# A two-block transformer kernel: small tables on another queue, two opening transposes and the modulation sums read later, modulation items shifted within the first mixer

## The chip, the cores and the metric

The kernel runs on one NeuronCore of a Trainium2 chip. Its engines are TensorE (PE, with weight loads PEld), VectorE (DVE), ScalarE (ACT), GpSimd (POOL) and SyncE (SP, which here only issues DMAs). The metric is the device time of one execution in microseconds (us), and the median of several runs is what is compared.

## What is computed

Two transformer blocks are applied one after the other to 256 tokens of width 2048, in float32. Each block gets six modulation vectors from a conditioning vector `c`: shift, scale and gate for the mixer and for the feed-forward part. The core of the reference, shortened:

```python
# first block
mod = silu(c) @ w_ada + b_ada                      # 2048 x 12288
sh_m, sc_m, gt_m, sh_f, sc_f, gt_f = split(mod, 6)
h = rmsnorm(x, pre_mix_norm) * (1 + sc_m) + sh_m
proj = h @ w_in
y = concat([hgrn2(proj[..., :HG_COLS]), gated_delta(proj[..., HG_COLS:])]) @ w_out
x = x + gt_m * rmsnorm(y, post_mix_norm)
h = rmsnorm(x, pre_ffn_norm) * (1 + sc_f) + sh_f
x = x + gt_f * rmsnorm(square(relu(h @ w_ff1)) @ w_ff2, post_ffn_norm)
# second block
u = rmsnorm(x, norm_mix_g) * (1 + sc1) + sh1       # its own mod, from c_2 and ada_w_2
x = x + g1 * hybrid_mixer(u)                       # fox, nsa, dilated and differential attention
u = rmsnorm(x, norm_ffn_g) * (1 + sc2) + sh2
x = x + g2 * ((silu(u @ w_gate) * (u @ w_up)) @ w_down)
out = rmsnorm(x, final_norm_g)
```

The differential attention needs one number, the lambda: `exp(sum(l0*l1)) - exp(sum(l2*l3)) + 0.2`.

## The kernel before

The program writes out one order of instructions by hand, with a small clock model of its own (`_Clock`, line 75) that estimates when each engine would be done. The model only chooses the order; the engines then run their queues in order and wait on semaphores.

**Items.** All large weights come as an ordered list `items` of 512 KB pieces. SyncE fetches each into one of five `raw` buffers (`dma_to`), and a buffer is free for the next piece when the piece has been used. A weight piece is split by `prep`: ScalarE rounds it to `wh` (fp32r), VectorE (or GpSimd) takes the rest `wl = raw - wh`, and TensorE multiplies `wh` and `wl` with the activations. A modulation piece (`ada`) lies between the weights. In its plain form VectorE multiplies it by one entry of silu(c) and adds it to a sum `acc` (one instruction of 128x1024, 16 pieces to a sum). In the other form (`cg`) TensorE sums two pieces at a time.

**Where the modulation items lie.** `weight(k)` gives each weight piece of block `k` a number; within a phase the modulation items are dealt out in proportion to the running sum of the numbers, so that they are through 24 units before the phase's end. The first phase goes from the first mixer to `("oA", 3)`. It deals 96 modulation items: 64 of the plain form for the scale and shift of the first feed-forward part, and 32 of the `cg` form for the mixer's gate. Its blocks are, for half 0, the last two pieces of each of `hq hf hv hg`, the small `ab`, and `zq zk zv gg`; for half 1 eight pieces of each of the same eight; then four `oA` blocks of six pieces (the output projection).

**Blocks and fills.** `run(b)` emits the matmuls of a block. After each step of 128 weight rows (each second one where a block has 256 columns) `fill` emits one step of the generator at the head of the queue `pri` (the block's own evacuation), one of `urgent`, up to two of `fillers` (attention, HGRN and gated-delta generators) and some `prep`. At its start `run` empties `pri` down to one generator by force; a step that emits nothing then pulls a filler forward. The second half's evacuation of `hq` waits until the HGRN generator of half 0 is through (`hg_done`).

**Sums.** When a sum has its last piece, `fin` puts a reader on `urgent`: `col_gen` transposes it on TensorE and adds it up on ScalarE, `row_gen` spreads it over the partitions. The reader may start 0.2 us, on the program's clock, after the sum. There are two `acc` buffers.

**Opening blocks.** The first block of each feed-forward part (`f1` 0,0 and `ga` 0,0) has its result with tokens on the partitions; `ev_relu2_s` and `ev_gate2_s` take it out of PSUM for one tile of 128 tokens, yield twice, transpose it on TensorE, and go on with the second tile. All later blocks of the part are computed transposed and need no such step.

**Second mixer.** After `run_first(blocks["fv"], ...)` the program emits the small tables on SyncE's queue (`fbias`, `cw2`, `cpos`), the lambda's DMA, its two VectorE instructions, the exponential on ScalarE and two more on VectorE into `nlam`; then `cmp_pre` fetches two tables `w1` of 512 KB in rows of 256 bytes (tiles `S` in the trace) on SyncE's queue, and `run(blocks["qG"])` starts. `nlam` is first read by `diff_gen`, after the block `fdv`.

Of the kernel before, what the change touches and what calls it, by code (L numbers as in the profile page):

```python
# [13 lines left out]
AF = mybir.ActivationFunctionType  # L14
ALU = mybir.AluOpType
AX = mybir.AxisListType
ADD, SUB, MUL, MAX = ALU.add, ALU.subtract, ALU.mult, ALU.max
# [161 lines left out]
def two_blocks(ctx, tc, I, out):  # L179
    nc = tc.nc  # L180
    PSUM = bass.MemoryType.PSUM
    clk = _Clock()
    pe, dve, act, pool, sync = (_Eng(clk, n, e) for n, e in (
        ("pe", nc.tensor), ("dve", nc.vector), ("act", nc.scalar), ("pool", nc.gpsimd), ("sync", nc.sync)))
# [6 lines left out]
    def row_bcast(ap, n):  # L191
        return bass.AP(tensor=ap.tensor, offset=ap.offset, ap=[[0, 128], [1, n]])
# [20 lines left out]
    def wt(name="wt"):  # L213
        return w2.tile([128, 512], F32, name=name, tag="wt")
# [4 lines left out]
    def small(shape, tag):  # L219
        n = 1 if tag in ONE or tag[:2] in ("sp", "sq", "cm") else 2 if tag[-1] in "01" and tag[:2] in ("ss", "rk", "rq", "s1", "sv") else 4  # L220
        return sm.tile([128] + shape, F32, name=tag, tag=tag, bufs=n)
# [9 lines left out]
    accs = {}  # L231
# [189 lines left out]
    def pri_step():  # L421
        q = pri.popleft()
        try:
            next(q)
        except StopIteration:
            return
        pri.appendleft(q)
# [21 lines left out]
    def add(q, before=0.0):  # L449
        lead[q] = before  # L450
        fillers.append((clk.t["pe"], q))
# [54 lines left out]
    def banks():  # L506
        return [psg.tile([128, 512], F32, name="g", tag="g") for _ in range(2)]
# [55 lines left out]
    def add_acc(b, pts, out):  # L563
        for p, a, o in zip(pts, b.acc, out):
            dve.tensor_tensor(o, p, a, op=ADD)

    def run(b):
        while len(pri) > 1:
            clk.end = 0.0
            pri_step()  # L570
            if not clk.end:
                fill_step(True)
        pts = b.pts or banks()
        run_units(b, pts, b.idx, len(b.kts) - sum(items[i]["nk"] for i in b.idx))
        if b.acc:
            add_acc(b, pts, b.acc)
            add(b.done(b.acc))
        elif b.done:
            pri.append(b.done(pts))
# [69 lines left out]
    g = {"hp": hpool}  # L649
# [141 lines left out]
    def ada_vecs(blk, vs, key=None, mul=False, cg=False):  # L791

        if cg:
            groups = [((v, q),) for q in range(4) for v in vs]
        elif len(vs) == 2:
            groups = [tuple((v, q) for v in vs) for q in range(4)]
        else:
            groups = [((vs[0], q), (vs[0], q + 1)) for q in (0, 2)]
        for vq in groups:
            def fin(vq=vq):  # L800
                for v, q in vq:
                    at = clk.wr[clk.key(accs[blk, v, q][0])][0] + 0.2
                    urgent.append((at, col_gen(blk, v, q) if key is None else row_gen(blk, v, q, key, mul)))
            n = 8 if cg else 16
            for k in range(n):
                ADA.append((blk, vq, k, fin if k == n - 1 else None, key is not None, cg))
# [623 lines left out]
    def ev_relu2_s(pts):  # L1430
        new_r(0)
        for t in range(2):
            r = wt("relu")
            act.activation(r, pts[t], AF.Relu)
            dve.scalar_tensor_tensor(r, pts[t], 0.0, r, op0=MAX, op1=MUL)
            yield
            yield
            p = mx()
            for j in range(4):
                pe.transpose(p[:, j * 128:(j + 1) * 128], r[:, j * 128:(j + 1) * 128], ident)  # L1440
            h, l = (x[:, :, t * 128:(t + 1) * 128] for x in rT[0])
            p4 = p.rearrange("p (a b) -> p a b", a=4)
            act.activation(h, p4, AF.Copy)
            dve.tensor_sub(l, p4, h)
# [196 lines left out]
    def cmp_pre():  # L1641
        g["cx2"], g["cw1"], g["cslots"] = [], [], []
        for i in range(2):
            k, S = s_slot()
            g["cslots"].append(k)
            x2, w1 = S[:, 0:544].rearrange("p (g t) -> p g t", g=2), S[:, 544:1568].rearrange("p (l e) -> p l e", l=16)
            g["cx2"].append(x2)
            g["cw1"].append(w1)
            sync.dma_start(w1, I["nsa_cmp_w1_2"][0, i].rearrange("(l p) e -> p l e", p=128))
            pool.memset(x2[:, :, 255:272], 0.0)  # L1650

    def cmp_mid():
# [250 lines left out]
    def ev_gate2_s(pts):  # L1903
        for t in range(2):
            th = wt("th")
            act.activation(th, pts[t], AF.Tanh, scale=0.5)
            dve.scalar_tensor_tensor(th, th, 1.0, pts[t], op0=ADD, op1=MUL)
            yield
            yield
            p = mx()  # L1910
            for j in range(4):
                pe.transpose(p[:, j * 128:(j + 1) * 128], th[:, j * 128:(j + 1) * 128], ident)
            act.activation(g["sg2"][:, 0, :, t * 128:(t + 1) * 128], p.rearrange("p (a b) -> p a b", a=4), AF.Copy)
            yield
# [27 lines left out]
    def weight(k):  # L1942
        if k[0] in ("oB", "pB") or k == "fv" or k in (("f1", 0, 0), ("ga", 0, 0)) or k[:3] in (("f1", 0, 1), ("f2", 3, 2), ("f2", 3, 3)):
            return 0.0
        if k in ("qG", "kvH", "sv"):
            return 0.5
        return 1.0

    LOW = {k: 1 for k in ("qG", "kvH", "sv", "qA", "kB", "qC", "kD", "dv0", "dv1", "qE", "kF", "fdv")}
# [26 lines left out]
    for endkey, ntot in phases:  # L1976
# [5 lines left out]
        for k in order[lo:hi]:  # L1982
            b = blocks[k]
# [77 lines left out]
    for b, o in zip(wide[1:], ("hk", "hv", "hg", "oh1", "ol1", "oh2", "ol2")):  # L2061
        a = g[o] if o in g else oTp.tile([128, 2, 512], F32, name="part", tag=o)
# [137 lines left out]
    b = blocks["f2", 3, 3]  # L2200
# [30 lines left out]
    g["cw2"] = mp.tile([128, 128], F32, name="cw2")  # L2231
    g["cpos"] = mp.tile([128, 128], F32, name="cpos")
    g["cposT"] = mp.tile([128, 32], F32, name="cposT")
    sync.dma_start(g["fbias"], row_bcast(I["fox_f_bias_2"][0], 7))
    for i in range(2):
        sync.dma_start(g["cw2"][0:64, i * 64:(i + 1) * 64], I["nsa_cmp_w2_2"][0, i])
    sync.dma_start(g["cpos"][0:32], I["nsa_cmp_pos_2"][0].rearrange("i (a l) d -> (i a) (l d)", l=2))
    lam = wt("lam")
    lamp = lam[:, 256:384].rearrange("p (a d) -> p a d", a=2)
    lam = lam[:, 0:256]  # L2240
    sync.dma_start(lam, row_bcast(I["diff_lambda_2"][0], 256))
    lam4 = lam.rearrange("p (a b d) -> p a b d", a=2, b=2)
    lams = small([2], "lams")
    dve.tensor_tensor(lamp, lam4[:, :, 0], lam4[:, :, 1], op=MUL)
    dve.tensor_reduce(lams, lamp, axis=AX.X, op=ADD)
    act.activation(lams, lams, AF.Exp)
    dve.tensor_sub(g["nlam"], lams[:, 1:2], lams[:, 0:1])
    dve.tensor_scalar(g["nlam"], g["nlam"], -(0.8 - 0.6), None, op0=ADD)
    for i in range(3):
        oT[i] = tuple(oTp.tile([128, 4, T], FR, name=f"o2{a}{i}", tag=f"o{a}{i}") for a in "hl")  # L2250
    cmp_pre()
# [2 lines left out]
        run(blocks[n])  # L2254
    drain(lambda: g.get("nsa_done") == 4)
    run(blocks["qE"])
    run(blocks["kF"])
    drain(lambda: g.get("fox_done") == 4)
    g["fdv"] = cpool.tile([128, 2, 512], F32, name="fdv", tag="v4")
# [32 lines left out]
    b = blocks["pB", 0]  # L2292
# [64 lines left out]
    b = blocks["dn", 2, 3]  # L2357
# [48 lines left out]
```

## Time and profile before

| | |
|---|---|
| median of 3 runs | 2776.14 us (2774.57 to 2776.25) |
| the profiled execution | 2775.45 us, span 2773.7 us |
| TensorE busy | 2635.9 us, 95% |
| VectorE, ScalarE, GpSimd busy | 65%, 45%, 15% |
| moved by DMA | 643.59 MB, mean 232 GB/s |

The page of the profile shows the busy time of each engine and, in forty slices, how it is spread. The views used below are: busy time by stretch, with the TensorE clock that was granted (1.00 is 2.4 GHz, 0.50 is 1.2 GHz) and the share of time that the 16 DMA engines were busy; the list of waits; and the timeline of one engine, in which a bracket at the end of a row says how long the engine had been idle and what ended that. Nearly all instructions come from one helper and carry its line, L169, so rows are told apart by the names of tiles.

### The profile page before, as it was taken

Reading aid. Unit: us, or ns where it says so; the run is one execution under the profiler, and the core shown is the slowest. Engines: PE = TensorE matmul, PEld = TensorE weight load, DVE = VectorE, ACT = ScalarE, POOL = GpSimd, SP = SyncE. Lnnn points to the kernel's source line nnn. Section 1 sums busy time; section 2 is a strip of 40 time slices with the busy share of each in tenths; the row PEclk is TensorE's granted clock in tenths of the full one; section 3 lists DMA queues with packets and bytes.
Section 4 is the critical chain, followed back from the end, with each engine's and each line's share of the span. In section 5 each row is a group of like instructions: output and inputs, shape, how many; then the busy total and the mean of one; then the engine's idle time right before and its main releaser. Section 6 shows DMA issues by size and latency. Waiting matters only on the chain.

```text
span 2773.7 us, 39578 instructions
## 1 busy us (share of the span) xinstructions
PE 2635.9 (95%) x15073; PEld 2211.8 (80%) x15073; DVE 1808.2 (65%) x2245; ACT 1259.4 (45%) x2124; POOL 409.7 (15%) x264
## 2 busy tenths in 40 slices
PE   7998879999989999999999799998999999999998
PEld 4887768869758788887887698986768888888887
DVE  3567957764667777887855346567867756654566
ACT  3433344344554454444454336454454444443443
POOL 1000141231000000000001465663400000000001
PEclk9999989999999999999999999999999999999999
DMA  9977858782568988989965674667767777666664
GB/s 362 314 256 243 222 148 252 229 250 92 197 203 274 319 287 298 316 278 326 307 205 163 201 219 157 219 225 239 240 192 239 238 245 224 198 190 190 190 189 144
DMA packets 399806, 643.59 MB, mean 232 GB/s; under 512 B 31480, under 2 KB 198088, under 8 KB 398208
## 3 DMA queue, kind: packets, MB, share of 16 engines
q1 hardware_dynamic: 396528, 628.26, 71.2%
q10 hardware_dynamic: 2336, 10.42, 1.0%
q8 instruction: 118, 1.93, 0.3%
q0 software_dynamic: 752, 2.39, 0.2%
q14 instruction: 72, 0.59, 0.1%
HBM read 636.27 MB, written 4.19 MB: 231 GB/s over the span
## 4 chain that ended last, share of the span: by engine, by line
PE 56%; DMA 6%; DVE 5%; ACT 2%; issue 2%; POOL 1%; SPq 0%; ACTq 0%; POOLq 0%; DVEq 0%
PE g L169 53%; DMA raw<-in_w_ff_dram 4%; PE mx L169 3%; DVE wl L169 2%; ACT wh L169 2%; POOL wl L169 1%; DMA raw<-in_w_in_dram 1%; DVE acc L169 1%; DMA raw<-in_w_out_dram 1%; DVE y L169 1%; DVE xres L169 0%; DMA raw<-in_ffn_w_up_dram 0%; ACT S L169 0%; SPq L169 0%; DVE S L169 0%
## 5 line engine op out<-in xcount | busy, mean ns | idle before, releaser
L169 PE MATMUL g<-hT,wh 128*128 128x512 f32 (+1 forms) x4448 | 1221.4, 345 | 19.7 <-ACT wh L169 17.7
L169 ACT ACTIVATE wh<-raw 128x1024 fp32r<-128x1024 f32 (+2 forms) x793 | 823.4, 1045 | 903.8 <-PE g L169 447.9
L169 DVE TENSOR_TENSOR wl<-raw,wh 128x1024 fp32r<-128x1024 f32 x691 | 858.4, 1249 | 527.1 <-ACT wh L169 519.8
L169 PE MATMUL g<-hT,wl 128*128 128x256 f32 x3376 | 956.2, 283 | 18.4 <-DVE wl L169 12.5
L169 PEld LDWEIGHTS g<-hT,wh 128*128 128x128 f32 x4448 | 773.2, 191 | 145.6 <-issue 23.6
L169 PEld LDWEIGHTS g<-hT,wl 128*128 128x128 f32 x3376 | 644.5, 191 | 23.6 <-DVE wl L169 14.8
L169 DVE SCALAR_TENSOR_TENSOR acc<-raw,csil,acc 128x1024 f32<-128x1024 f32 x276 | 381.6, 1383 | 75.1 <-DMA raw<-in_ada_w_dram 72.3
L169 PE MATMUL g<-wh,rh 128*128 128x512 f32 x864 | 339.9, 393 | 0.0
L169 PE MATMUL g<-wl,rh 128*128 128x512 f32 x864 | 339.6, 393 | 0.0
L169 PE MATMUL g<-wh,rl 128*128 128x512 f32 x864 | 339.2, 393 | 0.0
L169 POOL TENSOR_TENSOR wl<-raw,wh 128x1024 fp32r<-128x1024 f32 (+2 forms) x102 | 238.0, 2343 | 210.2 <-ACT wh L169 192.5
L169 PEld LDWEIGHTS g<-wh,rl 128*128 128x128 f32 x864 | 162.8, 188 | 36.3
L169 PEld LDWEIGHTS g<-wh,rh 128*128 128x128 f32 x864 | 162.7, 188 | 36.0
L169 PEld LDWEIGHTS g<-wl,rh 128*128 128x128 f32 x864 | 162.8, 188 | 35.5
L169 PE MATMUL g<-wh,hT 128*128 128x512 f32 (+2 forms) x544 | 162.0, 369 | 2.5 <-DVE hk L169 2.2
L169 PEld LDWEIGHTS g<-wh,hT 128*128 128x128 f32 x544 | 98.0, 190 | 22.4 <-issue 8.9
L169 POOL TENSOR_TENSOR y<-yy,gw 128x512 f32<-128x512 f32 x6 | 7.6, 1292 | 711.5 <-DVE yy L169 711.5
L169 PE MATMUL g<-wl,hT 128*128 128x512 f32 (+2 forms) x272 | 98.7, 363 | 3.2 <-DVE wl L169 2.2
L169 POOL TENSOR_TENSOR y<-y,gw 128x512 f32<-128x512 f32 x6 | 9.6, 1625 | 552.2 <-DVE y L169 547.0
L169 PE MATMUL g<-raw,y 128*128 128x512 f32 (+1 forms) x192 | 83.9, 580 | 2.8 <-DVE y L169 2.6
L169 PE MATMUL ada<-raw,csil 128*32 128x512 f32 x384 | 64.2, 647 | 10.6 <-DMA raw<-in_w_ada_dram 9.0
L169 PEld LDWEIGHTS g<-raw,y 128*128 128x128 f32 x192 | 34.6, 190 | 36.8 <-issue 30.0
(453 smaller groups left out, 2583.4 us busy)
## 6 DMA issues: line engine op xcount, KB each, us to landing
raw<-in_w_ff_dram SPq DMA_DIRECT2D x256, 512.0 KB, 5.4
raw<-in_w_ada_dram SPq DMA_DIRECT2D x192, 512.0 KB, 5.7
raw<-in_ada_w_dram SPq DMA_DIRECT2D x192, 512.0 KB, 5.0
raw<-in_w_in_dram SPq DMA_DIRECT2D x176, 512.0 KB, 5.6
raw<-in_ffn_w_gate_dram SPq DMA_DIRECT2D x88, 512.0 KB, 4.5
raw<-in_ffn_w_up_dram SPq DMA_DIRECT2D x88, 512.0 KB, 4.7
raw<-in_ffn_w_down_dram SPq DMA_DIRECT2D x88, 512.0 KB, 4.4
raw<-in_w_out_dram SPq DMA_DIRECT2D x60, 512.0 KB, 5.0
```

Source lines behind the costliest of these rows:

```text
L169: r = f(out, *a, **kw)
```

## The change

The tables `fbias`, `cw2`, `cpos` and `w1` are issued on ScalarE's queue instead of SyncE's. The lambda becomes a generator among the fillers, added after block `qE`, with its DMA on ScalarE's queue and twelve yields between the DMA and the first use. Both opening evacuations yield seven times instead of twice before they transpose. Readers of plain sums may start 5.0 us after the sum instead of 0.2; for `cg` sums it stays 0.2. In the first phase the pieces of half 0 (and `ab`) weigh 0, those of `hq` and `hf` of half 1 0.5, those of `oA` 1.5, and all others 1 as before.

```diff
@@ ada_vecs
-                    at = clk.wr[clk.key(accs[blk, v, q][0])][0] + 0.2
+                    at = clk.wr[clk.key(accs[blk, v, q][0])][0] + (0.2 if cg else 5.0)
@@ ev_relu2_s, and the same in ev_gate2_s
-            yield
-            yield
+            for _ in range(7):
+                yield
             p = mx()
@@ cmp_pre
-            sync.dma_start(w1, I["nsa_cmp_w1_2"][0, i].rearrange("(l p) e -> p l e", p=128))
+            act.dma_start(w1, I["nsa_cmp_w1_2"][0, i].rearrange("(l p) e -> p l e", p=128))
@@ weight(k)
+        if k == "ab" or k[1:] == (0,) and k[0] in ("hq", "hf", "hv", "hg", "zq", "zk", "zv", "gg"):
+            return 0.0
+        if k in (("hq", 1), ("hf", 1)):
+            return 0.5
+        if k[0] == "oA":
+            return 1.5
         return 1.0
@@ the start of the second mixer
-    sync.dma_start(g["fbias"], row_bcast(I["fox_f_bias_2"][0], 7))
+    act.dma_start(g["fbias"], row_bcast(I["fox_f_bias_2"][0], 7))
     for i in range(2):
-        sync.dma_start(g["cw2"][0:64, i * 64:(i + 1) * 64], I["nsa_cmp_w2_2"][0, i])
-    sync.dma_start(g["cpos"][0:32], I["nsa_cmp_pos_2"][0].rearrange("i (a l) d -> (i a) (l d)", l=2))
-    lam = wt("lam")
...
+        act.dma_start(g["cw2"][0:64, i * 64:(i + 1) * 64], I["nsa_cmp_w2_2"][0, i])
+    act.dma_start(g["cpos"][0:32], I["nsa_cmp_pos_2"][0].rearrange("i (a l) d -> (i a) (l d)", l=2))
+    def lam_gen():
+        lam = wt("lam")
+        lamp = lam[:, 256:384].rearrange("p (a d) -> p a d", a=2)
+        lam = lam[:, 0:256]
+        act.dma_start(lam, row_bcast(I["diff_lambda_2"][0], 256))
+        for _ in range(12):
+            yield
+        lam4 = lam.rearrange("p (a b d) -> p a b d", a=2, b=2)
+        lams = small([2], "lams")
+        dve.tensor_tensor(lamp, lam4[:, :, 0], lam4[:, :, 1], op=MUL)
+        dve.tensor_reduce(lams, lamp, axis=AX.X, op=ADD)
+        act.activation(lams, lams, AF.Exp)
+        yield
+        dve.tensor_sub(g["nlam"], lams[:, 1:2], lams[:, 0:1])
+        dve.tensor_scalar(g["nlam"], g["nlam"], -(0.8 - 0.6), None, op0=ADD)
@@ after run(blocks["qE"])
+    add(lam_gen())
     run(blocks["kF"])
```

## Rows read from the trace of the kernel before

**Rows 1.** The page, busy us, share of the span and instructions by engine.
```profile
PE 2635.9 (95%) x15073; PEld 2211.8 (80%) x15073; DVE 1808.2 (65%) x2245; ACT 1259.4 (45%) x2124; POOL 409.7 (15%) x264
```

**Rows 2.** Busy time by stretch: us, engines, then PEclk, DMA share, GB/s.
```profile
205.00:360.00 155.00, 129.96 (x930) 119.93 (x929) 136.35 (x190) 61.24 (x126) 18.95 (x12) 0.94 0.80 236
360.00:402.00 42.00, 28.99 (x151) 24.90 (x150) 17.62 (x32) 16.01 (x53) 20.38 (x18) 0.72 0.31 84
402.00:485.00 83.00, 79.10 (x483) 67.65 (x482) 63.04 (x82) 37.94 (x81) 18.45 (x13) 1.00 0.87 247
...
205.00:402.00 197.00, 158.94 (x1078) 144.83 (x1077) 153.97 (x221) 77.25 (x179) 39.34 (x29) 0.90 0.69 203
402.00:620.00 218.00, 210.05 (x1430) 172.68 (x1429) 152.88 (x227) 92.57 (x206) 54.55 (x41) 1.00 0.83 242
```

**Rows 3.** The same view, of the instructions that read or write `acc`.
```profile
205.00:360.00 155.00, 2.40 (x16) 1.85 (x16) 46.19 (x37) 0.00 (x0) 0.00 (x0) 0.94 0.80 236
```

**Rows 4.** Waits, us in total, times, longest: SyncE's queue 205:402, TensorE 205:350.
```profile
SPq L169 <- DVE acc L169: 75.5, 35, 5.3
...
PE g L169 <- DVE wl L169: 12.9, 9, 4.1
```

**Rows 5.** Timeline around the hole in SyncE's issues, and the first `oA` copy.
```profile
368.06 0.37 SPq L169 DMA_DIRECT2D raw<-in_w_in_dram  x1
402.76 0.37 SPq L169 DMA_DIRECT2D raw<-in_w_ada_dram  x1
...
397.17 1.08 ACT L169 ACTIVATE hq<-g 128x512 f32<-128x512 f32 x2
...
683.79 1.07 ACT L169 ACTIVATE y<-g 128x512 f32<-128x512 f32 x2
```

**Rows 6.** Timeline of TensorE, ScalarE and SyncE at the second mixer's start.
```profile
1564.09 0.80 PE L169 MATMUL g<-hT,wh 128*128 128x256 f32 x2 [10.36 <-ACT wh L169]
...
1547.28 1.06 ACT L169 ACTIVATE wh<-raw 128x1024 fp32r<-128x1024 f32 x1 [4.74 <-DMA raw<-in_w_in_dram]
1560.93 0.20 ACT L169 ACTIVATE lams<-lams 128x2 f32<-128x2 f32 x1 [12.59 <-DVE lams L169]
...
1550.81 2.02 SPq L169 DMA_DIRECT2D raw<-in_w_in_dram  x4
1552.88 0.60 SPq L169 DMA_DIRECT2D fbias<-in_fox_f_bias_dram  x1
1553.52 1.21 SPq L169 DMA_DIRECT2D cw<-in_nsa_cmp_w_dram  x2
1554.77 0.61 SPq L169 DMA_DIRECT2D cpos<-in_nsa_cmp_pos_dram  x1
1555.43 0.42 SPq L169 DMA_DIRECT2D lam<-in_diff_lambda_dram  x1
1556.02 3.91 SPq L169 DMA_DIRECT2D S<-in_nsa_cmp_w_dram  x2
```

**Rows 7.** Busy time by stretch there, columns as in rows 2.
```profile
1554.00:1556.00 2.00, 0.00 (x0) 0.00 (x0) 0.00 (x0) 0.00 (x0) 0.00 (x0) 1.00 1.05 393
...
1558.00:1560.00 2.00, 0.00 (x0) 0.00 (x0) 0.00 (x0) 0.00 (x0) 0.00 (x0) 0.50 0.89 220
...
1568.00:1570.00 2.00, 2.00 (x12) 2.00 (x11) 2.00 (x3) 0.32 (x2) 0.66 (x1) 0.53 0.99 314
```

**Rows 8.** Timeline of ScalarE and TensorE at the two opening blocks' transposes.
```profile
796.71 1.06 ACT L169 ACTIVATE wh<-raw 128x1024 fp32r<-128x1024 f32 x1 [1.66 <-DMA raw<-in_w_ff_dram]
...
807.17 0.59 ACT L169 ACTIVATE relu<-g 128x512 f32<-128x512 f32 x1
...
809.30 1.12 PE L169 MATMUL mx<-c,relu 128*128 128x128 f32 x4 [5.99 <-DVE relu L169]
...
2053.60 0.66 PE L169 MATMUL mx<-c,th 128*128 128x128 f32 x4 [3.32 <-DVE th L169]
```

**Rows 9.** TensorE's waits over the whole span, for finished sums.
```profile
PE mx L169 <- DVE acc L169: 4.5, 3, 2.5
```

More of the change, by code (lines that the diff above doesn't have):

```diff
@@ L1907, in ev_gate2_s @@
             dve.scalar_tensor_tensor(th, th, 1.0, pts[t], op0=ADD, op1=MUL)
-            yield
-            yield
+            for _ in range(7):
+                yield
             p = mx()
@@ L2233, in two_blocks @@
     g["cposT"] = mp.tile([128, 32], F32, name="cposT")
-    sync.dma_start(g["fbias"], row_bcast(I["fox_f_bias_2"][0], 7))
+    act.dma_start(g["fbias"], row_bcast(I["fox_f_bias_2"][0], 7))
     for i in range(2):
-        sync.dma_start(g["cw2"][0:64, i * 64:(i + 1) * 64], I["nsa_cmp_w2_2"][0, i])
-    sync.dma_start(g["cpos"][0:32], I["nsa_cmp_pos_2"][0].rearrange("i (a l) d -> (i a) (l d)", l=2))
-    lam = wt("lam")
[L2239 to L2248, printed above, removed]
+        act.dma_start(g["cw2"][0:64, i * 64:(i + 1) * 64], I["nsa_cmp_w2_2"][0, i])
[12 more added lines that the diff above has]
+        act.activation(lams, lams, AF.Exp)
+        yield
+        dve.tensor_sub(g["nlam"], lams[:, 1:2], lams[:, 0:1])
+        dve.tensor_scalar(g["nlam"], g["nlam"], -(0.8 - 0.6), None, op0=ADD)
     for i in range(3):
```

## The prediction

> **What bounds the kernel now.** I read the page's busy line first: TensorE is busy 95% of the span, the other engines far less [rows 1]. Busy time alone has little to give back, so I looked for stages where TensorE is not busy or not at full clock: busy time by stage, then who waits for whom in it, then the timeline at each stop. Three places carry nearly all of it.
>
> The first is the opening of the first mixer's main loop, 205 to 402 us: TensorE is busy 158.94 of 197 us at a mean granted clock of 0.90 [rows 2]. That is 38 us idle, and 0.10 x 158.94 = 16 us of matmuls stretched by the half clock, 54 us in all. From 402 us on, up to 620, it is busy 210.05 of 218 at clock 1.00. In the opening VectorE is the fuller engine for most of the time: 136.35 of 155 us (88%) from 205 to 360. A third of that, 46.19 us in 37 instructions, is the modulation sums (`acc`) [rows 3]. The DMA queue shows the same: SyncE waits 75.5 us in 35 stops for VectorE to finish a sum before it may refill that raw buffer, and TensorE waits 12.9 us for low halves `wl` that VectorE makes [rows 4]. Then comes a stop of its own: SyncE issues nothing between 368.06 and 402.76 us, because the program runs out the HGRN chain before it goes on, and the gated-delta chain is emitted among it; ScalarE copies the second half's `hq` at 397.17 [rows 5]. In 360 to 402 the clock is 0.72.
>
> The second is the start of the second mixer: TensorE stands 10.36 us until 1564.09 because ScalarE's `wh` stand behind the exponential of the lambdas (1560.93), which stands behind a DMA that SyncE issued at 1555.43 [rows 6]. The third is two stops in front of transposes of the opening blocks, 5.99 and 3.32 us [rows 8]; three stops for finished sums add 4.5 us [rows 9].
>
> **Items shift within the first mixer.** No byte and no instruction is added. Working the weights through with the code: 96 sum items follow the first 64; the stage's weight falls from 81 to 68. Before, 21 of the 96 lie among half 0's blocks, 19 in `hq`, `hf` of half 1, 56 in `hv` to `gg`, none in `oA`. After: 0, 12, 68 and 16. So before `hv` of half 1, which starts near 402 us, 28 of 40 items go away: 28 x 1.25 us (46.19/37 [rows 3]) = 35 us less on VectorE, and 28 x 0.52 = 15 MB less to fetch. VectorE's 153.97 us in the opening become 119 [rows 2]. TensorE's own work at full clock is 0.90 x 158.94 = 143 us. With 119 beside 143, VectorE is 83% full; the nearest row is 402 to 485, VectorE 63.04 of 83 (76%), where TensorE lost 4 of 83 us, 5%. At 5 to 15% of 143 it loses 7 to 21 us in place of 54: a gain of 33 to 47, and I take 40. The stop at 368 to 402 goes with it because the HGRN and convolution steps, which queue on VectorE, end earlier than the weight blocks do; the chain's matmuls done in that stop are not saved, only laid between weight matmuls, and the 143 counts them.
>
> The 28 items come back later. Between 402 and 620 VectorE's 152.88 us grow by up to 35 to 188, or 86% of 218 [rows 2]. Its row for such a load is 205 to 360 (88%), where TensorE idled 25 of 155 us, 16%; that would cost 16% of 218 = 35 less the 8 lost there now, 27. But 16 of the items now lie in `oA`, and gate-vector items (32 of the 96) are summed by TensorE, not VectorE. I take a cost of 10, bounds 0 and 27. Net 30, bounds 6 and 47.
>
> **Lambdas and tables on ScalarE's queue.** The tables' six issues took 0.60, 1.21, 0.61 and 3.91 us on SyncE [rows 6], 6.3 us, which ScalarE now spends. It had ended a `wh` at 1548.34 and then stood for the exponential until 1560.93. So it would be through its issues at about 1554.7 and copy `fv` by 1555.7, which the old stall covers; without that cover those 6.3 us would be on the path. What is next late is the weights: four raw tiles were issued from 1550.81, 2.1 MB, and moved at 393 GB/s [rows 7], about 5.4 us, the first landing near 1555. Then one `wh` of 1.06 us and a low half: TensorE goes on near 1557 to 1560 instead of 1564, a gain of 4 to 7. Bounds: nothing, if the tables' 1.05 MB in small rows (220 GB/s in 1558 to 1560, when they moved) come first, 4.8 us; and 10.4 plus some 2 us of half clock, which lasted to about 1569.5 (0.53 in 1568 to 1570 [rows 7]). I take 6. The lambda's DMA, two VectorE and one ScalarE instructions move behind `qE`; twelve turns of the filler queue pass between issue and first use, one a fill at most, so nothing waits for its landing.
>
> The Trainium skill ("DMA: Bandwidth & Descriptors", section "Issuing engines are not separate DMA queues") says that transfers started by ScalarE and SyncE run on the same 16 engines and interleave, so a second issuer saves only issue time. The trace has the engines at a share of 1.05 while the four tiles moved [rows 7], so they had no room for tables beside them; by the rule alone this part gives 1 or 2 us and the sum would be 38 or 39 instead of 43.
>
> **Transposes later.** In `f1` the stop of 5.99 us ends at 809.30, when ScalarE's `relu` of the second token tile (807.17) and a VectorE product are through [rows 8]. Seven turns instead of two put the first tile's transposes at the end of the next block (8 fills) and the second tile's at the head of the one after, where `run` empties the queue by force. TensorE can use the stop for the block's remaining matmuls, whose weights `wh` began at 796.71 were long there. But the second tile is evacuated only at that eighth fill, so at the boundary TensorE waits for `relu` 0.59, the product 0.68 and what stands before them: 1.4 us at least, up to 4.6 with two `wh` and `wl` ahead. I take 3, a gain of 3. In the gate block likewise 3.32 against about 2: a gain of 1. Together 4; bounds -2 (both waits come back a little longer) and 9.3 (both gone).
>
> **Sums read later.** Column and row readers start 5.0 instead of 0.2 us, on the program's own clock, after a sum. That can remove at most the three stops of 4.5 us [rows 9]; TensorE has matmuls ready in each. A buffer is held longer, but the next user of the same buffer is 16 items on. I take 3; bounds -1 and 4.5.
>
> **Sum.** 30 + 6 + 4 + 3 = 43 us. The profiled execution took 2775.45 us (span 2773.7 and 1.75 around it), 0.7 under the median 2776.14. 2775.45 - 43 = 2732.4, against the median 2733; I say 2733.
>
> **Rivals.**
> - *The chain sets the opening, not VectorE.* The HGRN steps hand over between TensorE, VectorE and GpSimd; with VectorE free the blocks `hq`, `hf` come through faster and TensorE only waits longer for the same chain. For it: in 360 to 402 VectorE was busy 17.62 of 42 us and TensorE still stood [rows 2]. Against it: before 360 VectorE was 88% busy. The opening would then give back about half, 25 less 10 later; with 13 of the other parts 28 us or, with those at half, 20: about 2750 to 2756, I say 2753.
> - *The later stage pays all (slower).* From `hv` to the second `oA` block 84 items and 56 weight units, 73 MB, must come through five raw buffers that VectorE or TensorE empties. They now have from 402 to about 691: the first `oA` block, six of the eight units, is copied out at 683.79 [rows 5]. That is 289 us, and some 303 with the gated-delta matmuls that move in. At the 242 GB/s of 402 to 620 the bytes take 303 us, at the 236 of the VectorE-bound 205 to 360 [rows 2] 311: little or nothing is lost. The other side is 54 + 13 = 67 us at the very most, so from about 205 GB/s down (358 us, 69 more than 289) the kernel is slower; at 200 (367, 78 more) it takes 2787. For it: five buffers refill no faster than VectorE, fuller here than before, frees them. Against it: the share was 0.83 at 242 GB/s, and the second half of the stretch is not full of VectorE work.
> - *All at the upper bounds*: 47 + 12 + 9 + 4 = 72, 2704.
> - *It doesn't do what it says*: the program orders work by a clock of its own, and the later items are forced early by the two `acc` buffers, or stalls only change their name. Then within 5 us of 2776.
>
> **How the numbers follow.** Chances: forecast (2715 to 2745) 0.50; chain 0.24; upper bounds 0.10; no change 0.08; slower 0.08. From 2704 to 2772 all but the slower case, the no-change case and the tail below 2704 are held, about 0.80. About 0.2%, 5.5 us, is what a measurement of this kernel can tell from no change. Faster 0.84, same 0.08, slower 0.08.
>
> **What would show it.** In the new trace: `hq` of half 1 copied near 340 to 360 instead of 397; VectorE's sums before it down to about 12; no 34 us hole in SyncE's issues; clock near 1.00 from 205 on; VectorE 80 to 87% full in the two hundred microseconds behind, with TensorE still over 93% busy there. At the second mixer a stop of 3 to 6 us, ended by a weight DMA, not by the lambdas. In `f1` a stop of about 3 us at a block boundary. The forecast is wrong if the hole before `hv` stays, or if TensorE's waits for raw weights between `hv` and `oA` grow by more than 20 us.

## The result and the profile after

| | before | after |
|---|---|---|
| median | 2775.36 us (2774.15 to 2776.25) | 2759.52 us (2756.43 to 2761.39) |
| the profiled execution, its span | 2775.45, 2773.7 us | 2756.43, 2754.7 us |

The ratio is 0.9935, 95% interval 0.9923 to 0.9948: 16 us or 18 us faster, by medians or by ratio. The forecast was 43 us, 2733. The direction was right, the size well under half.

Busy time by stretch after, columns as in rows 2; the first three and the next two answer [rows 2], the last two are the opening up to the copy of `hq` of half 1 and the way from there to the first feed-forward part:

```profile
205.00:360.00 155.00, 140.53 (x1014) 130.54 (x1014) 121.42 (x187) 72.50 (x137) 33.84 (x24) 0.96 0.63 171
360.00:402.00 42.00, 37.79 (x193) 30.60 (x192) 32.94 (x38) 17.41 (x45) 14.17 (x9) 0.92 0.86 250
402.00:485.00 83.00, 81.01 (x620) 76.74 (x619) 73.28 (x93) 32.92 (x74) 24.11 (x15) 0.98 0.84 230
205.00:402.00 197.00, 178.32 (x1206) 161.13 (x1206) 154.36 (x224) 89.92 (x182) 48.01 (x33) 0.95 0.68 188
402.00:620.00 218.00, 204.15 (x1437) 174.01 (x1436) 166.66 (x242) 90.85 (x222) 63.79 (x46) 0.98 0.86 251
...
205.00:349.60 144.60, 132.90 (x978) 124.35 (x977) 114.69 (x175) 65.02 (x125) 29.82 (x21) 0.95 0.67 183
349.60:740.30 390.70, 366.52 (x2296) 307.16 (x2296) 270.57 (x388) 171.86 (x378) 92.76 (x68) 0.98 0.75 224
```

The same two stretches of the kernel before:

```profile
205.00:397.20 192.20, 154.27 (x1062) 140.85 (x1060) 153.06 (x219) 73.03 (x173) 38.44 (x29) 0.91 0.71 208
397.20:763.00 365.80, 352.48 (x2204) 294.14 (x2204) 230.41 (x341) 163.02 (x331) 75.91 (x60) 0.99 0.67 202
```

The timeline after, of the rows that answer [rows 5], [rows 6] and [rows 8]:

```profile
336.23 0.37 SPq L169 DMA_DIRECT2D raw<-in_w_ada_dram  x1
358.07 0.37 SPq L169 DMA_DIRECT2D raw<-in_w_in_dram  x1
...
349.65 1.11 ACT L169 ACTIVATE hq<-g 128x512 f32<-128x512 f32 x2
...
664.01 1.08 ACT L169 ACTIVATE y<-g 128x512 f32<-128x512 f32 x2
...
790.56 0.69 PE L169 MATMUL mx<-c,relu 128*128 128x128 f32 x2 [5.84 <-DVE relu L169]
...
1519.46 1.58 ACTq L169 DMA_DIRECT2D S<-in_nsa_cmp_w_dram  x2
1520.64 1.95 SPq L169 DMA_DIRECT2D raw<-in_w_in_dram  x4
...
1526.76 1.06 ACT L169 ACTIVATE wh<-raw 128x1024 fp32r<-128x1024 f32 x1 [3.60 <-DMA raw<-in_w_in_dram]
...
1527.87 0.39 PE L169 MATMUL g<-hT,wh 128*128 128x256 f32 x1 [4.31 <-ACT wh L169]
...
2041.33 0.90 PE L169 MATMUL mx<-c,th 128*128 128x128 f32 x3 [8.92 <-DVE th L169]
```

To see where the time went, the same event is looked up in each trace. Each number is the start of that copy on ScalarE minus its start in the kernel before, in us; the columns behind "after" are experiments told below. Each column is one execution, and executions of one kernel differ by some microseconds, so a step of 3 us in one column means little by itself; one that comes back in several columns means more.

| copy (start before) | after | items | tables | sums | transposes | both tiles |
|---|---|---|---|---|---|---|
| `hq` of half 1 (397.17) | -47.5 | -48.9 | +0.7 | -2.6 | +0.6 | -48.0 |
| first `oA` (683.79) | -19.8 | -16.7 | +0.8 | -3.3 | +0.2 | -15.7 |
| last of `f1` (1421.78) | -29.9 | -22.6 | +0.2 | -11.4 | +3.4 | -30.2 |
| last `dv` (1803.16) | -35.3 | -23.3 | -10.1 | -7.2 | +4.0 | -39.5 |
| last `qE` (1838.64) | -30.5 | -23.6 | -9.8 | -3.7 | +4.4 | -39.7 |
| `fdv` (1894.49) | -27.0 | -23.8 | -6.3 | -4.0 | +4.5 | -36.3 |
| first `th` of the gate block (2051.59) | -25.8 | -24.7 | -6.8 | -4.3 | +3.8 | -36.1 |
| last `y` of the first down-projection (2298.23) | -18.9 | -24.7 | -8.3 | -4.7 | +10.8 | -40.2 |

The "after" column is a ledger. The opening gives some 20 to 23 us, the sums in `f1` and `f2` another 7, the second mixer's start 5. At `dv` the kernel is 35 us ahead, not far from the forecast's 43. Then it loses: 8 us from `dv` to `fdv`, and 7 more at the gate block.

### The profile page after: what moved, and what is told of

It is laid out like the page before. It is cut to its first block, busy times and chain, and to the rows that moved or that the text cites. A ratio compares the mean times of both kernels' runs of the same rounds, so it can differ in the third digit from the quotient of the medians.

```text
span 2754.7 us, 39576 instructions
## 1 busy us (share of the span) xinstructions
PE 2629.3 (95%) x15073; PEld 2207.5 (80%) x15073; DVE 1814.2 (66%) x2247; ACT 1260.8 (46%) x2124; POOL 410.0 (15%) x262
## 4 chain that ended last, share of the span: by engine, by line
PE 59%; DMA 4%; DVE 4%; POOL 2%; issue 2%; ACT 2%; SPq 0%; POOLq 0%; ACTq 0%; DVEq 0%
PE g L169 56%; PE mx L169 3%; POOL wl L169 1%; DMA raw<-in_w_in_dram 1%; DMA raw<-in_w_out_dram 1%; DVE wl L169 1%; DMA raw<-in_w_ff_dram 1%; ACT wh L169 1%; DVE acc L169 1%; DVE y L169 1%; DVE xres L169 0%; DMA raw<-in_ffn_w_up_dram 0%; DMA raw<-in_ada_w_dram 0%; DMA raw<-in_ffn_w_gate_dram 0%; DVE S L169 0%
## 5 line engine op out<-in xcount | busy, mean ns | idle before, releaser
L169 PEld LDWEIGHTS g<-hT,wh 128*128 128x128 f32 x4448 | 772.9, 191 | 125.8 <-issue 18.9
L169 POOL TENSOR_TENSOR wl<-raw,wh 128x1024 fp32r<-128x1024 f32 (+2 forms) x100 | 230.1, 2311 | 222.7 <-ACT wh L169 211.2
```

The source lines that it names most:

```text
L169: r = f(out, *a, **kw)
```

## The experiments

Ratios are against the kernel before, run on the same chip beside it (medians there 2771 to 2776).

| kernel | ratio, 95% interval | median, us |
|---|---|---|
| items alone | 0.9914 (0.9895 to 0.9933) | 2752.1 |
| tables and lambda alone | 0.9981 (0.9969 to 0.9994) | 2769.6 |
| sums alone | 0.9984 (0.9973 to 0.9996) | 2770.6 |
| transposes alone | 1.0036 (1.0023 to 1.0049) | 2785.4 |
| changed, old transposes | 0.9924 (0.9901 to 0.9947) | 2752.1 |
| and sums split | 0.9894 (0.9871 to 0.9917) | 2742.7 |
| and both tiles at once | 0.9864 (0.9839 to 0.9889) | 2734.1 |
| and lambda early | 0.9844 (0.9822 to 0.9867) | 2728.2 |
| before, sums narrow on the chip | 0.9956 (0.9939 to 0.9972) | 2760.7 |
| before, sums narrow in the clock | 0.9949 (0.9931 to 0.9967) | 2758.5 |
| before, narrow in both | 0.9916 (0.9901 to 0.9931) | 2748.4 |
| and fetched narrow | 0.9940 (0.9923 to 0.9956) | 2754.4 |
| before, fillers ahead | 1.0099 (1.0085 to 1.0114) | 2803.0 |
| lambda early, fillers ahead | 0.9969 (0.9959 to 0.9979) | 2766.4 |
| the same, old item weights | 0.9995 (0.9982 to 1.0008) | 2773.0 |
| items alone, sums narrow in the clock | 0.9938 (0.9919 to 0.9956) | 2756.8 |
| lambda early, sums narrow in the clock | 0.9841 (0.9821 to 0.9861) | 2729.8 |

**Each part alone.** Four kernels take over one part of the change each; their edits are hunks of the diff above.

Items:

> The kernel before with only the new weights for the modulation items. Theory A (each part has its own price, and the ledger by stage of the changed kernel's trace holds them): the first oA copy comes 18 to 22 us earlier, the first feed-forward part begins 20 to 24 us earlier, and the time is 2751 to 2757. Theory B (the forecast's 30 is right for this part, and something else eats it later in the changed kernel): the feed-forward part begins 28 to 33 us earlier, 2743 to 2748.

Tables and lambda:

> The kernel before with only the tables and the lambda moved to ScalarE's queue and the lambda made a later generator. Theory A (the lost ten microseconds of the second mixer belong to the late sums): the gain at the second mixer's start, 6 us, stays to the end: 2769 to 2771. Rival C (they belong to the lambda's generator, which runs among the kF block's attention steps): the gain of 6 us is gone again by the block after kF, and the time is 2775 to 2779.

Sums:

> The kernel before with only the later readers of plain sums (5.0 instead of 0.2). Theory A: 5 to 8 us gained in the first block's feed-forward part, where TensorE no longer stops for sums, and 5 to 10 us lost in the second mixer, where the readers fall among the attention steps: 2773 to 2781. Rival C (the second mixer's loss isn't theirs): 2768 to 2771.

Transposes:

> The kernel before with only seven yields instead of two in both opening evacuations. Theory A (the second tile of the gate block is now evacuated at the head of the next block, behind four weight roundings): about 0 in f1 and 5 to 7 us lost at the gate: 2780 to 2783. The forecast's value: 4 us gained, 2772. Rival C (the stop only changes its name, weights are what is late at both places): 2775 to 2777.

By the medians the four are worth 22, 4, 3 and -11 us (against 2773.97): 18 together, and the whole change 16 to 18. So the parts add up, within intervals of some 3 to 5 us either way for each. Theory A of the expectations holds for the first three in the places of gain and loss; for the sums its time does not (2770.6 lies in rival C's range). The transposes cost more than any theory had: 3 us stand by the end of `f1`, and 7 more at the gate block.

In the table of events the sums gain 8 us between `oA` and the end of `f1`, and lose 8 from there to `qE`: both places of theory A. The lambda's rival C is partly right too: from `qE` to `fdv` the tables' column falls from -9.8 to -6.3, with TensorE waiting 3.8 us for attention's VectorE steps in the `kF` block. The table repeats this in each kernel that has the lambda behind `qE` (after, tables, both tiles: 3.4 or 3.5 us lost there) and in no other (items, sums, transposes: 0.1 at most).

**The gate's transposes and the second mixer's sums, in the changed kernel.**

```diff
@@ ev_relu2_s, ev_gate2_s (old transposes, on the changed kernel)
-            for _ in range(7):
-                yield
+            yield
+            yield
```

> The changed kernel with both opening evacuations back at two yields. If the later transposes cost here what they cost alone (11 us on the kernel before), the stop before the gate block's second transposes falls from 8.9 us to about 3, and the time is 2746 to 2751. If the cost belongs to their meeting with the other parts, nothing is regained: 2757 to 2760.

2752.1 us, between the two expectations and nearer the first. That is 7 us less than the changed kernel by the medians and 3 by the ratios, whose intervals overlap. In the traces the loss of the gate block (7 us from its first `th` to the last `y`) is gone and the stop there is 2.29 us instead of 8.92, so that loss was the transposes'; the 11 us that they cost alone are not all regained.

```diff
@@ ada_vecs (sums split, on top)
-                    at = clk.wr[clk.key(accs[blk, v, q][0])][0] + (0.2 if cg else 5.0)
+                    at = clk.wr[clk.key(accs[blk, v, q][0])][0] + (0.2 if cg or blk == 1 and v in (2, 4, 5) else 5.0)
```

> The same, and the readers of the sums that finish in the second mixer and after it (scale of its feed-forward part, g1 and g2) may start 0.2 after the sum again, those before keep 5.0. If the late readers cost the second mixer its stop of 5.3 us before the kD scores, that stop falls under 2 us, and the time is 4 to 8 us under the kernel with old transposes: 2740 to 2745. If the lambda's generator is the cause, it is the same as that kernel within 2 us.

2742.7 us: 9 us less, and the stop before the `kD` scores goes from 5.44 us in the kernel with the old transposes to 0.50. This is that stop in the changed kernel, TensorE, then VectorE and GpSimd ahead of it:

```profile
1775.28 1.04 PE L169 MATMUL mx<-kD,qC 64*128 64x128 f32 x3 [5.33 <-DVE S L169]
...
1766.50 2.35 DVE L169 TENSOR_TENSOR colt<-red,cols 128x4 f32<-128x4 f32 x1
1768.88 2.27 DVE L169 SCALAR_TENSOR_TENSOR Affn<-colt,cols 128x4 f32<-128x4 f32 x1
1771.07 1.27 DVE L169 SCALAR_TENSOR_TENSOR acc<-raw,csil,acc 128x1024 f32<-128x1024 f32 x1
1772.27 2.29 DVE L169 TENSOR_TENSOR colt<-red,cols 128x4 f32<-128x4 f32 x1
...
1766.08 5.04 POOL L169 TENSOR_TENSOR wl<-raw,wh 128x1024 fp32r<-128x1024 f32 x2 [0.60 <-ACT wh L169]
1771.56 2.98 POOL L169 TENSOR_TENSOR wl<-raw,wh 128x1024 fp32r<-128x1024 f32 x1 [0.43 <-ACT wh L169]
```

and with the sums split:

```profile
1768.84 0.84 PE L169 MATMUL mx<-kD,qC 64*128 64x128 f32 x3 [0.50 <-DVE S L169]
```

In the changed kernel the late readers stand in VectorE's queue in front of the scores, and three of their four 128x4 instructions last until GpSimd's subtraction beside them ends.

**Both tiles at once.**

```diff
@@ ev_relu2_s (ev_gate2_s alike)
-        for t in range(2):
+        rs = []
+        for t in range(2):
             r = wt("relu")
             act.activation(r, pts[t], AF.Relu)
             dve.scalar_tensor_tensor(r, pts[t], 0.0, r, op0=MAX, op1=MUL)
+            rs.append(r)
+        for _ in range(4):
             yield
+        for t, r in enumerate(rs):
             yield
```

> The same, and the opening evacuations take both token tiles out of PSUM at once, then yield, then transpose the first and at the next step the second. If the stops of 5.8 and 3.3 us come from the second tile's evacuation standing behind the next block's weight roundings on ScalarE, both vanish, the next weights are late instead by up to 4 us in all, and the time falls by another 4 to 8 us: 2733 to 2740. If weights are what is late there anyhow, the stops only take their name, and the time stays within 2 us.

2734.1 us, another 9 less. These are TensorE's transposes, each row the first of its group, and none has a bracket: the stops (5.67 and 2.19 us in the kernel before this step, 5.84 and 8.92 in the changed kernel) are gone, and TensorE has no other stop in their place. On ScalarE both `th` (x2) now stand ahead of the roundings:

```profile
785.41 0.60 PE L169 MATMUL mx<-c,relu 128*128 128x128 f32 x4
...
2019.13 0.49 PE L169 MATMUL mx<-c,th 128*128 128x128 f32 x3
...
2022.39 0.38 PE L169 MATMUL mx<-c,th 128*128 128x128 f32 x2
...
2015.51 1.06 ACT L169 ACTIVATE th<-g 128x512 f32<-128x512 f32 x2
2016.46 2.05 ACT L169 ACTIVATE wh<-raw 128x1024 fp32r<-128x1024 f32 x2
```

**Lambda early.**

```diff
     add(fox_pre())
+    add(lam_gen())
...
     run(blocks["qE"])
-    add(lam_gen())
```

> The kernel with both tiles evacuated at once, and the lambda's generator added at the start of the second mixer instead of behind qE. If its steps cost the kF block the 3 us that the stage lost with the tables alone (9.8 us ahead after qE, 6.3 after fdv), that loss goes and the time falls by 2 to 4 us against the kernel with both tiles. If the lambda's exponential stands in ScalarE's queue ahead of weights at the mixer's start again, it is 3 to 6 us slower. If neither, within 1.5 us.

2728.2 us, the fastest of all here by its median. The intervals of this and the last kernel overlap, so for the whole time the place of the lambda is not shown to matter. For its stretch the traces show it. From the copy of `qE` to that of `fdv` the five kernels with the lambda behind `qE` take 59.3 to 59.5 us (after, tables, old transposes, sums split, both tiles). All others take 55.4 to 56.0, whether the lambda is where it was before or early, but for this one, which takes 56.9: its wait in the `kF` block fell only from 4.0 to 3.2 us.

**What bounded the opening.** The forecast said VectorE. To part its time from the order of the steps, the first sums are narrowed to 64 columns on the chip, in the program's clock, or in both. Where they are narrow on the chip, the kernel leaves out the other 960 columns of these sums, so its result is incomplete; it serves for its time alone.

```diff
@@ prep (all three; it counts the plain pieces)
+            st["plain"] = st.get("plain", 0) + 1
             if k == 0 and not it["row"]:
                 dve.tensor_scalar(a, it["raw"], sc, None, op0=MUL)
+            elif st["plain"] <= 40:
...
@@ narrow on the chip alone
+                nc.vector.scalar_tensor_tensor(a[:, 0:64], it["raw"][:, 0:64], sc, a[:, 0:64], op0=MUL, op1=ADD)
+                clk.run("dve", "scalar_tensor_tensor", a, [it["raw"], sc, a], [])
@@ narrow in both
+                dve.scalar_tensor_tensor(a[:, 0:64], it["raw"][:, 0:64], sc, a[:, 0:64], op0=MUL, op1=ADD)
@@ narrow in the clock alone
+                nc.vector.scalar_tensor_tensor(a, it["raw"], sc, a, op0=MUL, op1=ADD)
+                clk.run("dve", "scalar_tensor_tensor", a[:, 0:64], [it["raw"][:, 0:64], sc], [])
@@ dma_to (fetched narrow, on top of narrow in both)
+                if not it["cg"] and k and st["fetched"] <= 40:
+                    sync.dma_start(raw[:, 0:64], src[:, 0, 0:64])
```

On the chip alone:

> The kernel before, with 38 of the first 40 VectorE sum instructions reduced to 64 of their 1024 columns (the rest of these sums is left out, so the first feed-forward part's modulation is incomplete); all bytes are still fetched, all instructions keep their order. This takes some 42 us from VectorE in the opening and nothing from the DMA engines. If VectorE's time is what bounds the opening, hq of half 1 is copied at 345 to 360 instead of 397 and the time falls by 30 to 40 us, to 2735 to 2745. If the raw buffers' bytes bound it, hq comes at 385 or later and the time is over 2765; if the HGRN hand-overs bound it, in between.

In both:

> As the narrow sums (same sums left out beyond their first 64 columns, all bytes fetched, SyncE's order unchanged), but now the program's own clock also counts them as narrow, so it emits the HGRN and gated-delta steps earlier. If the order that the clock made was what kept hq of half 1 behind in the narrow sums (387 instead of the 350 of the changed kernel), hq comes at 345 to 362 and the time falls below 2750. If the bytes of the 28 items set it, hq stays at 380 to 390 and the time within 5 us of the narrow sums' 2760.

In the clock alone:

> The kernel before with all sums computed in full, but the program's clock counts the first 38 as narrow: only the order in which the steps are emitted changes, neither VectorE's work nor bytes. If VectorE's time and the order both count, hq of half 1 comes 5 to 20 us earlier than 397 and the time falls by 3 to 12 us. If the order alone decides, it falls by as much as with the narrow sums in both. If VectorE's time alone decides, within 3 us of the kernel before, or slower.

In both, and the pieces fetched narrow as well:

> As narrow in both, and of these 38 pieces only 64 of 1024 columns are fetched too (what is left out is the same): the bytes of the first 40 sum pieces all but vanish, 18 MB less. If bytes bound the opening, hq of half 1 comes at 340 to 355 here where narrow in both leaves it at 380 or later. If not, the two differ by less than 8 us at hq.

Busy time by stretch, first narrow on the chip alone:

```profile
205.00:360.00 155.00, 136.95 (x989) 125.48 (x988) 110.29 (x205) 66.53 (x147) 20.29 (x18) 0.96 0.85 253
360.00:402.00 42.00, 32.53 (x150) 28.26 (x148) 14.80 (x25) 18.96 (x46) 18.72 (x15) 0.63 0.22 62
```

SyncE's issues in it:

```profile
356.48 0.37 SPq L169 DMA_DIRECT2D raw<-in_w_in_dram  x1
393.05 0.37 SPq L169 DMA_DIRECT2D raw<-in_w_ada_dram  x1
```

and busy time by stretch, narrow in the clock alone:

```profile
205.00:360.00 155.00, 132.69 (x938) 122.50 (x936) 135.88 (x194) 62.02 (x127) 18.37 (x13) 0.94 0.81 237
360.00:402.00 42.00, 35.90 (x159) 27.20 (x159) 33.78 (x38) 23.28 (x65) 19.31 (x14) 0.92 0.92 251
```

On the chip alone the result lies between the readings of its expectation; in the clock alone `hq` came 34 us earlier, more than the 5 to 20 expected. With 26 us less work on VectorE up to 360 (110.29 against 136.35 [rows 2]), TensorE gains 7 us there, but the hole of SyncE stays (36 us) and the stretch from 360 to 402 is as bad as before. With VectorE as full as before and only the order of the steps another, that stretch is mended. Each is worth some 12 to 14 us, both together 23: on the kernel before the two causes add, within the intervals. `hq` comes at 387 (on the chip), 363 (in the clock) and 353 (in both). Fetching 18 MB less on top brought nothing (2754.4), so no run here shows the bytes to be the bound. It does not exclude them either: the order of steps shifts in that kernel too, the hole is back (34 us) and `hq` comes at 381, so the expected 8 us at most was missed.

Does simply emitting those steps sooner do it?

```diff
@@ fill_step (on the kernel before)
-            if force or at <= clk.t["pe"] + lag[0]:
+            if force or at <= clk.t["pe"] + (6.0 if "gg" in g and "hg_done" not in g else lag[0]):
```

> The kernel before, unchanged but for one rule of the emission: until the HGRN generator of half 0 is through, a filler step may be emitted up to 6 us before the program's clock calls it ready, instead of 0. No sum, no byte and no item moves, and SyncE's order is the same. If the opening's stop exists because these steps are written behind the weight work and then run out by force, SyncE's hole of 34 us goes or shrinks below 15, hq of half 1 comes 25 to 45 us earlier and the time falls by 12 to 25 us. If the narrow model gained for another reason (its sums' places), the hole stays and the time is within 5 us of the kernel before.

> The kernel with old item weights undone nowhere: both tiles evacuated at once, sums split, lambda early, new item weights, and the same 6 us rule. The changed kernel's own hole of 21 us before 358 and its stop of 6.0 us for hgA should shrink; if they do and nothing is late next, the time is 2 to 10 us under the kernel with the early lambda. If the steps now stand in front of weight work on VectorE, it is the same or up to 5 us slower.

> The same without the new item weights (the modulation items lie as in the kernel before). If the shift of the items mostly bought an order of steps, this is within 8 us of the same kernel with the new weights; if moving VectorE's 35 us is worth most of it, it is 12 to 25 us slower than that.

No. In the first the hole is gone and `hq` comes 24 us earlier, and yet it is 27 us slower: TensorE now stands in front of the steps themselves. Its wait for `hq` on VectorE from 205 to 402 us is new, that for `wl` was 14.2 us before; and up to 360 its granted clock is 0.80, where it was 0.94 [rows 2]:

```profile
PE mx L169 <- DVE hq L169: 12.9, 5, 5.6
PE g L169 <- DVE wl L169: 10.9, 13, 2.2
...
205.00:360.00 155.00, 117.10 (x692) 105.09 (x691) 103.92 (x148) 46.39 (x92) 18.39 (x15) 0.80 0.55 167
```

The rule spoils the fastest kernel too (2766.4), and with it the old and the new item weights are 7 us apart, which by the expectation speaks for the order of steps as most of what the shift bought. But both kernels lost much to the rule itself, so this is weak evidence. Neither the hole nor the time of `hq` is a price by itself: emitting the steps 6 us ahead removes the hole and loses more elsewhere. The expected gain of 12 to 25 us did not come. Whether a smaller lead would gain was not tried.

Last, whether the shift has already bought the order:

> Only the new item weights, as in the items alone (0.9914 of before), and the program's clock counts the first 38 full sums as narrow, which on the old item order gave 0.9949 by the order of steps alone. If the shift of the items bought the opening by the order of steps that it let the clock make, the two don't add: 0.990 to 0.993, 2746 to 2756. If it bought it by VectorE's time, they add: about 0.986, 2735 to 2740.

> The kernel with both tiles evacuated at once, sums split, early lambda and new item weights (0.9844 of before), and the same narrow count in the program's clock. By the same two readings: 0.983 to 0.987 if the order is already bought, 0.979 to 0.981 if the two add.

They don't add: 0.9938 and 0.9841 against 0.9914 and 0.9844 (the first is a little above the range expected for that). This fits a shift that already holds what the order alone gave, but it doesn't show it. In the shifted kernel only 16 plain sums run before `hq`, and the 40th starts at 450.8 us, where the kernel before had it at 364.4. So most of the narrow count falls behind the opening there and changes another stretch, and how much of the shift's gain is order stays open.

## Why the prediction was right and wrong, step by step

**The step that failed: transposes later.** The forecast was a gain of 4, bounds -2 to 9.3; it is a loss, 11 us alone (ratio 1.0036, interval 1.0023 to 1.0049). For `f1` the mechanism was foreseen (the second tile's evacuation at the last fill, the transposes at the block's head), but its price was not: 5.84 us remain of 5.99 [rows 8], not 3, since the forecast had "two `wh` and `wl` ahead" at most, where five `wh` run between the two `relu`, the first after a wait of 6.04 us for its weights (ScalarE, in the changed kernel):

```profile
781.04 1.06 ACT L169 ACTIVATE wh<-raw 128x1024 fp32r<-128x1024 f32 x1 [6.04 <-DMA raw<-in_w_ff_dram]
...
788.43 0.59 ACT L169 ACTIVATE relu<-g 128x512 f32<-128x512 f32 x1
```

"In the gate block likewise" was wrong. Its generator has one more yield, at the end of each tile, so with seven the second tile's evacuation itself, not only its transposes, falls to the head of the next block. There ScalarE's queue already holds that block's roundings, which wait for their weights:

```profile
2032.60 1.06 ACT L169 ACTIVATE wh<-raw 128x1024 fp32r<-128x1024 f32 x1 [3.88 <-DMA raw<-in_ffn_w_up_dram]
2033.98 1.06 ACT L169 ACTIVATE wh<-raw 128x1024 fp32r<-128x1024 f32 x1 [0.33 <-DMA raw<-in_ffn_w_up_dram]
2035.43 1.06 ACT L169 ACTIVATE wh<-raw 128x1024 fp32r<-128x1024 f32 x1 [0.39 <-DMA raw<-in_ffn_w_gate_dram]
2036.39 0.58 ACT L169 ACTIVATE sg<-mx 128x512 f32<-128x512 f32 x1
2038.37 1.06 ACT L169 ACTIVATE wh<-raw 128x1024 fp32r<-128x1024 f32 x1 [1.39 <-DMA raw<-in_ffn_w_gate_dram]
2039.33 0.58 ACT L169 ACTIVATE th<-g 128x512 f32<-128x512 f32 x1
```

The last line is the second tile's `th`; TensorE stands 8.92 us for it, where it stood 3.32. Taking both tiles at once, with the transposes still five and six steps later, removed both stops. So late transposes do no harm by themselves; what cost the time was the second tile's evacuation behind the next block's roundings on ScalarE. Alone this term is 15 us of the 25 to 27 that are missing; in the changed kernel, where going back to the old transposes regained 3 to 7, it is 7 to 11.

**Items shift: right in kind, 6 to 8 us too high, and for part of the reason.** Net 30 was forecast; alone it is 22 to 24. Up to `hq` of half 1 the kernel before loses 192.2 - 0.91 x 154.27 = 52 us, the changed one 144.6 - 0.95 x 132.90 = 18: inside the 7 to 21 expected, but at its upper end, a gain of 34 instead of 40. From there to the feed-forward part it was 365.8 - 0.99 x 352.48 = 17 and is 390.7 - 0.98 x 366.52 = 32: a cost of 15 instead of 10 (a hundredth of clock is 3.7 us of the last product, so neither is known better than that). Part of the cost has a name: TensorE's waits for `wl` on that way went from 0.8 to 7.7 us. That is less than the 20 us of waits for weights that the prediction had as a sign of being wrong.

The signs came true in part: `hq` at 349.65, sums of 21.23 us instead of 46.19 [rows 3] up to 360, but a hole of 22 us remained, where none was forecast, and the clock was 0.95, not 1.00. VectorE behind was 76% full (166.66 of 218), less than the 80 to 87 expected, with TensorE at 94%. The sentence that failed is that the stop before `hv` "goes with it because the HGRN and convolution steps, which queue on VectorE, end earlier": on the kernel before, with the sums narrow on the chip alone, VectorE had 26 us less to do and the hole stayed. There VectorE's load is about half of the cause, and the other half is the order of the HGRN and gated-delta steps that the program's clock makes of it. Whether the shift's own gain splits the same way is not shown, and which step has to lie where is not settled. Of the 47 us at `hq`, some 14 were work put off (0.91 x 154.27 = 140 us of full-clock matmuls up to it before, 0.95 x 132.90 = 126 now) and 34 were won, of which up to 15 were lost again behind it.

**Lambdas and tables: right.** Forecast 6, bounds 0 to 12; 4 to 8 us alone. The stop is 4.31 us instead of 10.36 and its end is a `wh` that waited for weights, as the forecast had it. The 1 or 2 us that the prediction worked out from the Trainium skill's rule ("DMA: Bandwidth & Descriptors", section "Issuing engines are not separate DMA queues") did not come: the tables were issued on ScalarE's queue just before SyncE's four tiles (the two `w1`, `S`, from 1519.46), the first `wh` starts 6.1 us after the tiles' issue (1520.64 to 1526.76), and the stop still shrank by 6.0. This doesn't contradict that the transfers share their engines. ScalarE no longer stands for the lambda, as it did for 12.59 us [rows 6]; no run moves the tables without the lambda, so the 6 us are not parted between them. What was missed is the lambda's new place: "nothing waits for its landing" is right, but its steps lie among the `kF` block's attention, and 3.5 us go between `qE` and `fdv` in each kernel that has it there. Put early, it gave back 2.4 us of them in one profile and all in three others, though the whole time does not show it.

**Sums read later: the sum right, both sides missed.** Forecast 3; alone 3.4. Yet TensorE's waits for `acc` [rows 9] are gone, and `f1` and `f2` gained 8 us with the sums alone, twice the stops (4.8 of idle time and 3.3 of busy time for the same matmuls, at a clock of 1.00 instead of 0.99); and the second mixer lost about as much. "TensorE has matmuls ready in each" holds for the feed-forward parts and not for attention, where a step of VectorE stands between two of TensorE's. The error is a bound that took only the stops in view, and no look at whom the readers stand before when they come late.

**The rivals.** "The chain sets the opening" (2753) came nearest in time. Its mechanism is close to what the kernel before did with the sums narrow on the chip alone: TensorE gained 7 us up to 360 and then, up to 402, did no more full-clock work than before (0.63 x 32.53 = 20 us, against 0.72 x 28.99 = 21). It is not what the changed kernel did, where TensorE was busy 37.79 of the 42 us from 360 to 402. (28 us off 2776 is 2748, so its own range reached lower than the 2750 that it gives.) The slower case did not come; 402 to 620 us moved 251 GB/s, over the 242 that the estimate needed.

## What to carry to other kernels

When a step is moved later in a hand-written order, list what is then queued ahead of it on its own engine, and estimate its wait from that list, not from the gap that it leaves. A milestone that comes earlier proves nothing while work has been put off past it: subtract the full-clock work from the elapsed time on both sides of it. And where an order comes from a program's own cost model, taking work away changes the order as well; part the two by changing the model alone.

## What the hardware showed

VectorE's 128x4 instructions, as short as 0.15 to 0.16 us elsewhere in the same trace, took 2.27 to 2.35 us in three of four cases in front of the `kD` scores, and ended within 0.03 us of GpSimd's subtraction of 128x1024 beside them: `Affn` at 1768.88 + 2.27 = 1771.15 and GpSimd's pair at 1766.08 + 5.04 = 1771.12; the second `colt` at 1774.56 and GpSimd's third at 1774.54. The Trainium skill ("SBUF — State Buffer", section "🔬 SBUF: two separate sides") says that the two engines' shared port pair is an exclusive lock held for a whole instruction, taken by a VectorE instruction with two SBUF inputs against a GpSimd one that reads SBUF. The trace agrees: what a VectorE step costs in the second mixer depends on what GpSimd runs beside it, up to fifteen times its own time.
